# K and V of the first octet in rows of 4 KB: four transfers for two, and a branch of TensorE's loop for their sums

## The chip, the cores and the metric

The kernel runs on one core of a Trainium2 chip. The metric is the device time of one execution in microseconds (us), as the median of several runs. Engines are named as in the profile: PE (TensorE, matrix products), DVE (VectorE), ACT (ScalarE), POOL (GpSimd) and SP (SyncE, which here only issues transfers). Sixteen DMA engines move the data between HBM and the core's memory (SBUF); PE writes its results into PSUM.

## The reference

Linear attention with ReLU features, for 8 x 12 = 96 heads of 512 rows by 64 columns, all in float32:

```python
Q_feat = np.maximum(0, Q)                                   # Q, K, V: (8, 12, 512, 64)
K_feat = np.maximum(0, K)
KV = np.einsum('bhkd,bhkv->bhdv', K_feat, V)
K_sum = np.sum(K_feat, axis=2)
numerator = np.einsum('bhqd,bhdv->bhqv', Q_feat, KV)
denominator = np.einsum('bhqd,bhd->bhq', Q_feat, K_sum)
out = numerator / (denominator[:, :, :, None] + 1e-10)
```

Each head needs a 64 x 64 sum over its 512 keys, the sum of its keys, and then a product of its queries with both.

## The kernel before

**Tiles.** The 96 heads are taken in 12 octets of 8 heads (`NO = 12`). The view `Kr[o]` (and `Qr`, `Vr`, `Or`) is one octet of 1 MB, laid on 128 partitions with 32 rows of 64 numbers each (`RQ = 32`), which is one run of 8 KB per partition. A head thus covers 16 partitions.

**Loads.** Pool's queue loads Q, K and V and casts them to bf16 on the way (`load`, L174): 8 KB read and 4 KB written per row. Each input has `NI = 6` octets of buffers, and Pool's transfers take six semaphores (`lanes`) in turn; a transfer waits until the one before it on its lane has landed. Some transfers bring two octets. Only K and V of octet 0 come another way: SP issues them as they are, in float32, into the output buffers `o_sb[0]` and `o_sb[1]` (L267), each with a lane of its own. The helper `lane` deals out lanes in turn.

**Order.** There is no scheduler. `Order.op` (L58) records each instruction with the keys that it reads and writes, and adds the semaphore waits that follow from them. A transfer writes the key of its lane too (L65), so that a second transfer on a lane waits for the first. PE's work is a loop over `r` (L384), whose waits are written by hand and booked by `do.looped`.

**Per octet.** DVE turns K into masked features (`prep_k`, L191): for each row `kf` has two copies of 64 columns, one holding it where the partition belongs to an even head of a pair, the other where it belongs to an odd one. `prep_v` (L200 on ACT, L202 on DVE) does the same for V by a mask over 32 partitions, beside columns of ones. PE transposes Q (L389), multiplies for the denominators and numerators of the octet before (L382), sums K times V (L413), and transposes the numerators back (L422). The sums of an octet are 64 products over half of the partitions each: for each of 32 rows one over partitions 0 to 63 and one over 64 to 127, into two columns of banks of `ps_kv`. ACT copies the blocks on the diagonal into `kvd` (`evac_kv`, L218). DVE divides (`norm`, L245) into `o_sb`.

**Stores.** SP stores an octet of 1 MB at a time (L254). Every store's keys hold K's buffer of octet 11 (L253), so the first store waits until that load has landed, and all twelve follow one another after it.

**Start.** `body` issues K and V of octet 0 on SP, then on Pool the first loads, the identity, a block of memsets (L263), and the loads of octets 2 to 5. `setup` makes the masks on DVE from the identity (L297 to L302) and prepares octet 0, `begin` does the first turn around PE's loop, and `step(i)` the rest.

Of the kernel before, what the change touches and what calls it, by code (L numbers as in the profile page):

```python
# [96 lines left out]
def kernel(  # L97
# [19 lines left out]
    NI = 6  # L117
# [15 lines left out]

    ident = sb.tile([P, P], bf16, name="ident")
    ident32 = sb.tile([P, P], fp32, name="ident32")
    mask = sb.tile([P, 2, 2], fp32, name="mask")
    mask_h = sb.tile([P, 8, 2], fp32, name="mask_h")
    kf = sb.tile([P, RQ, 2, D], bf16, name="kf")
# [27 lines left out]
    def kv_src(o):  # L166
        if o == 0:
            return (o_sb[0], ("o", 0)), (o_sb[1], ("o", 1))
        return [(ins[n][:, o % NI].rearrange("p (r d) -> p r d", d=D), (n, o % NI)) for n in "kv"]
# [18 lines left out]
    def prep_k(o, s, halves=(0, 1), after=()):  # L188
        src, key = kv_src(o)[0]
        rs = slice(R * halves[0], R * halves[-1] + R)  # L190
        do.op("dve", lambda e: e.tensor_scalar(kf[:, rs, s, :], src[:, rs], scalar1=0.0, scalar2=mask[:, 0, s:s + 1],  # L191
                                               op0=Alu.max, op1=Alu.mult),
              reads=[key, ("mask", 0), *after], writes=[("kf", s, j) for j in halves])

    def prep_v(o, t, halves, who, sem=None):
        src, key = kv_src(o)[1]
# [6 lines left out]
        do.op(who, make, reads=[key, ("mask", 1), "vo1"], writes=[("vo", t, j) for j in halves], sem=sem)  # L203
# [11 lines left out]
    def evac_kv():  # L215
        for s in range(2):
            for c in range(2):
                do.op("act", lambda e: e.copy(  # L218
                    kvd[64 * c:64 * c + 64, s:8:2, c * D1:c * D1 + D1].rearrange("p (g t) d -> p g t d", t=2),
# [22 lines left out]
    def norm(o, j):  # L242
# [4 lines left out]
              reads=[("x", j), "rec"], writes=[("o", i, j)] if i > 1 else [("o", i, j), ("o", i)], sem=f"n{j}")  # L247
# [17 lines left out]
    def body():  # L265
        for c, X in enumerate((Kr, Vr)):
            do.op("sp", lambda e: e.dma_start(out=o_sb[c].rearrange("p r d -> p (r d)"), in_=X[0]),  # L267
                  writes=[("o", c)], dma=lane("sp"))
# [27 lines left out]
    def setup():  # L296
        do.op("dve", lambda e: e.tensor_copy(ident32, ident), reads=["ident"], writes=["ident32"])  # L297
        for c in range(2):
            do.op("dve", lambda e: e.tensor_reduce(
                out=mask_h[:, :, c], in_=ident32.rearrange("p (h b) -> p h b", h=8), op=Alu.add,  # L300
                axis=mybir.AxisListType.X), reads=["ident32"], writes=[("mh", c), "mask_h"])
# [31 lines left out]
    def begin():  # L333
        transposed(1)
        relu_q(0)
        relu_q(1)
        summed(1)
        evac_kv()
        prep_v(1, 1, (0,), "act", "a0")
        prepare(1)  # L340
# [37 lines left out]
    def products():  # L378
# [4 lines left out]

        with pe.Fori(0, NO + 2, 1) as r, pe.If(r > 0):  # L384
            with pe.If(r < NO + 1):
                pe.wait_ge(sems["rq"], r)
                pe.wait_ge(sems["q2"], r)
                for u in range(U):
                    x = pe.transpose(ps_qt[u // 8][:, u % 8, :], q2[:, u, :], ident)  # L389
                    if u % 8 == 7:  # L390
                        x.then_inc(sems["pe"], 1)
            with pe.If(r > 1):
# [13 lines left out]
            with pe.If(r < NO + 1):  # L406
                for g in range(2):
                    for s in ("a0", "d0") if g == 0 else ("d1",):
                        pe.wait_ge(sems[s], r)
                    for k in range(R):  # L410
                        for h in range(2):
                            ps = slice(64 * h, 64 * h + 64)
                            x = pe.matmul(  # L413
                                ps_kv[:, h, 0:2 * (D + 2)].rearrange("p (t d) -> p t d", t=2),
                                kf[ps, R * g + k, :, :].rearrange("p s d -> p (s d)"), vo[ps, R * g + k, :, 1:D4 - 1],
                                start=(g + k == 0), stop=(g == 1 and k == R - 1), skip_group_check=True)
                    x.then_inc(sems["pe"], 1)
            with pe.If(r > 1):
# [45 lines left out]
```

## Time and profile before

| what | value |
|---|---|
| median of 3 runs | 125.11 us (125.01 to 125.23) |
| profiled execution, whole | 125.09 us |
| its span | 123.3 us |
| DVE busy | 84.3 us (68%) |
| PE busy / weight loads | 81.1 us (66%) / 72.3 us (59%) |
| ACT busy | 76.3 us (62%) |
| POOL busy | 25.6 us (21%) |
| SP's queue (q1): packets | 2016, 14.68 MB |
| Pool's queue (q0): packets | 4832, 17.83 MB |
| HBM | 37.75 MB read, 12.58 MB written, 408 GB/s over the span |

The profile shows one execution by the hardware profiler. The span is what it covers; the run's own time is 1.8 us more. The page has the busy time of each engine, a strip of 40 slices of the span with busy tenths (for DMA the mean busy share of the 16 engines), the DMA queues, the chain of work that ended last, and the costliest groups of instructions. Further views of the trace answer for a stretch of time: the windows view gives each engine's busy time in a stretch, then PE's granted clock, the DMA share and the GB/s that were written; the timeline lists instructions in order, with the idle time before them and what ended it in brackets; the waits view adds up who waited for whom (total, times, longest). The trace also records each DMA packet with its queue, size, start and duration.

### The profile page before, as it was taken

The page shows a single profiled execution, that of the slowest core. Times are in us where ns is not written, and L with a number is a line of the kernel's source. Part 1 is how long each engine was busy: PE and PEld are TensorE (multiplying, and loading weights), DVE is VectorE, ACT ScalarE, POOL GpSimd, SP SyncE. Part 2 cuts the span into 40 slices and gives each one's busy share as a digit, 9 for nine tenths or more (in the row PEclk, how much of TensorE's full clock was granted, in tenths as well). Part 3 has the DMA queues.
Part 4 walks back from the last instruction along what each step waited for, and adds up shares of the span by engine and source line. Part 5 has one row for each costly group of instructions (what it writes and reads, how often), then busy time and mean ns, then how long its engine had stood idle before and what let it go on. Part 6 is the DMA issues. An engine that isn't in the chain of part 4 may idle for free.

```text
span 123.3 us, 3456 instructions
## 1 busy us (share of the span) xinstructions
PE 81.1 (66%) x1440; PEld 72.3 (59%) x1440; DVE 84.3 (68%) x149; ACT 76.3 (62%) x108; POOL 25.6 (21%) x64
## 2 busy tenths in 40 slices
PE   0000089797599896989989898989898884800000
PEld 0000089697289794979889797979696763700000
DVE  1252933555999879999999999999979577520000
ACT  0000751994698889979899999999996963000000
POOL 5888922001111013213331222100000000000000
PEclk9999999999679999999999999999999998695555
DMA  2999999999999999999999999999999999999991
GB/s 64 392 314 237 213 214 215 213 214 213 213 214 214 217 214 214 213 214 214 213 215 215 213 213 214 214 214 213 213 302 423 425 423 428 425 423 430 428 430 74
DMA packets 6852, 32.55 MB, mean 264 GB/s; under 512 B 704, under 2 KB 704, under 8 KB 5056
## 3 DMA queue, kind: packets, MB, share of 16 engines
q0 software_dynamic: 4832, 17.83, 72.0%
q1 hardware_dynamic: 2016, 14.68, 28.7%
q8 instruction: 1, 0.02, 0.1%
q14 instruction: 3, 0.02, 0.0%
HBM read 37.75 MB, written 12.58 MB: 408 GB/s over the span
## 4 chain that ended last, share of the span: by engine, by line
DMA 54%; DVE 18%; PE 8%; issue 5%; POOL 3%; POOLq 0%; DVEq 0%; SPq 0%
DMA v_sb<-in_V_dram 22%; DMA k_sb<-in_K_dram 20%; DMA q_sb<-in_Q_dram 12%; DVE o_sb L245 9%; PE ps_x L422 4%; DVE kf L191 4%; PE ps_kv L413 3%; DVE vo L202 2%; POOL q_sb L174 2%; DVE own L231 1%; DVE ot_sb L226 1%; POOL k_sb L174 1%; DVE den L237 1%; DVE q L206 1%; DVE rec L240 0%
## 5 line engine op out<-in xcount | busy, mean ns | idle before, releaser
L245 DVE TENSOR_TENSOR o_sb<-ps_x,rec 128x1024 f32<-128x1024 f32 x24 | 28.5, 1218 | 5.0 <-PE ps_x L422 4.4
L413 PE MATMUL ps_kv<-vo,kf 64*128 64x132 bf16 x768 | 27.0, 229 | 4.7 <-DVE vo L202 4.6
L413 PEld LDWEIGHTS ps_kv<-vo,kf 64*128 64x128 bf16 x768 | 25.0, 99 | 7.8 <-issue 7.8
L422 PE MATMUL ps_x<-ident,ot_sb 128*128 128x128 f32 x192 | 25.0, 286 | 1.7 <-DVE ot_sb L226 1.7
L226 ACT COPY ot_sb<-ps_x 128x1024 f32<-128x1024 f32 x23 | 22.4, 1015 | 4.7 <-PE ps_x L382 4.3
L210 ACT ACTIVATE qt<-ps_qt 128x1024 bf16<-128x1024 bf16 x24 | 23.5, 1040 | 1.9 <-PE ps_qt L389 1.9
L389 PE MATMUL ps_qt<-ident,q 128*128 128x128 bf16 x192 | 13.7, 229 | 15.8 <-DVE q L206 15.8
L422 PEld LDWEIGHTS ps_x<-ident,ot_sb 128*128 128x128 f32 x192 | 22.1, 147 | 3.2 <-issue 2.0
L191 DVE TENSOR_SCALAR kf<-k_sb,mask 128x1024 bf16<-128x1024 bf16 x44 | 18.6, 482 | 5.8 <-DMA k_sb<-in_K_dram 3.6
L389 PEld LDWEIGHTS ps_qt<-ident,q 128*128 128x128 bf16 x192 | 12.5, 103 | 16.1 <-issue 16.0
L218 ACT CAST kvd<-ps_kv 64x260 bf16<-64x260 f32 x48 | 18.0, 376 | 3.4 <-PE ps_kv L413 2.6
L382 PE MATMUL ps_x<-qt,kvd 128*128 128x256 bf16 x96 | 14.2, 284 | 3.3 <-DVE o_sb L245 3.2
L200 ACT ACTIVATE vo<-v_sb,mask 128x1024 bf16<-128x1024 bf16 x11 | 12.7, 1155 | 3.9 <-DMA v_sb<-in_V_dram 3.7
L202 DVE TENSOR_SCALAR vo<-v_sb,mask 128x2048 bf16<-128x2048 bf16 (+1 forms) x22 | 12.6, 615 | 0.0
L382 PEld LDWEIGHTS ps_x<-qt,kvd 128*128 128x128 bf16 x96 | 7.9, 101 | 6.5 <-DVE o_sb L245 5.1
L174 POOL DMA_DIRECT2D v_sb<-in_V_dram x11 | 6.5, 588 | 22.2 <-DMA q_sb<-in_Q_dram 8.6
L206 DVE COPY q<-q_sb 128x2048 bf16<-128x2048 bf16 x12 | 7.7, 646 | 2.8 <-PE ps_qt L389 2.1
L174 POOL DMA_DIRECT2D k_sb<-in_K_dram x9 | 6.2, 685 | 15.5 <-DMA k_sb<-in_K_dram 10.3
L174 POOL DMA_DIRECT2D q_sb<-in_Q_dram x10 | 6.3, 632 | 13.9 <-DMA q_sb<-in_Q_dram 7.1
L200 ACT ACT_TABLE_LOAD x1 | 1.3, 1283 | 12.5 <-DMA o_sb<-in_V_dram 12.5
L382 PE MATMUL ps_kv<-kvd,qt 128*128 128x16 bf16 x192 | 7.0, 179 | 0.9 <-ACT kvd L218 0.9
L382 PEld LDWEIGHTS ps_kv<-kvd,qt 128*128 128x128 bf16 x192 | 6.2, 96 | 1.3 <-ACT kvd L218 1.3
(20 smaller groups left out, 29.5 us busy)
## 6 DMA issues: line engine op xcount, KB each, us to landing
out_dram<-o_sb SPq DMA_DIRECT2D x12, 1024.0 KB, 16.3
v_sb<-in_V_dram POOLq DMA_DIRECT2D x11, 512.0 KB, 15.6
q_sb<-in_Q_dram POOLq DMA_DIRECT2D x8, 512.0 KB, 14.5
k_sb<-in_K_dram POOLq DMA_DIRECT2D x7, 512.0 KB, 14.4
q_sb<-in_Q_dram POOLq DMA_DIRECT2D x2, 1024.0 KB, 17.0
k_sb<-in_K_dram POOLq DMA_DIRECT2D x2, 1024.0 KB, 20.4
o_sb<-in_K_dram SPq DMA_DIRECT2D x1, 1024.0 KB, 6.5
o_sb<-in_V_dram SPq DMA_DIRECT2D x1, 1024.0 KB, 11.0
```

The costliest lines, as they stand in the source:

```text
L174: do.op("pool", lambda e: e.dma_start(out=ins[n][:, i:i + m], in_=src, single_packet=True), writes=[(n, x % NI) for x in octets], dma=lane ...
L191: do.op("dve", lambda e: e.tensor_scalar(kf[:, rs, s, :], src[:, rs], scalar1=0.0, scalar2=mask[:, 0, s:s + 1], op0=Alu.max, op1=Alu.mult) ...
L200: make = lambda e: e.activation(to, src, Act.Copy, scale=m)
L202: make = lambda e: e.tensor_scalar(to, src, scalar1=m, scalar2=None, op0=Alu.mult)
L210: do.op("act", lambda e: e.activation(qt[:, j * (U // 2):(j + 1) * (U // 2)], ps_qt[j], Act.Relu), reads=[("pq", j)], writes=[("qt", j)], ...
L218: do.op("act", lambda e: e.copy(kvd[64 * c:64 * c + 64, s:8:2, c * D1:c * D1 + D1].rearrange("p (g t) d -> p g t d", t=2), ps_kv[64 * s:64 ...
L226: do.op(who, lambda e: e.copy(to, src) if who == "act" else e.tensor_copy(to, src), reads=[("x", j)], writes=[("ot", j)], sem=f"t{j}")
L245: do.op("dve", lambda e: e.tensor_tensor(o_sb[i][:, rs], ps_x[j].rearrange("p (r d) -> p r d", d=D), rec[:, rs].unsqueeze(2).to_broadcast( ...
L382: return pe.matmul(out_, lhsT, rhs, start=True, stop=True, skip_group_check=True)
L389: x = pe.transpose(ps_qt[u // 8][:, u % 8, :], q2[:, u, :], ident)
L413: x = pe.matmul(ps_kv[:, h, 0:2 * (D + 2)].rearrange("p (t d) -> p t d", t=2), kf[ps, R * g + k, :, :].rearrange("p s d -> p (s d)"), vo[p ...
L422: x = pe.transpose(ps_x[u // 8][:, u % 8 * P:u % 8 * P + P], ot[:, u].rearrange("p h c -> p (h c)"), ident32)
```

## The change

K and V of octet 0 are seen through another view, `Kf` and `Vf`: four heads on 128 partitions, 16 rows (4 KB) on each. Two transfers of 0.5 MB fill the two halves of `o_sb[0]` for K, two more those of `o_sb[1]` for V. The lanes are written out: both halves of K on `sl0`, V's on `sl1` and `sl2`. As a head now covers 32 partitions in octet 0, its K mask is `mask_f` (halves of 64 partitions), and the sums of a group of four heads run over all 128 partitions: 32 products in a branch of its own in PE's loop for `r < 2`, ahead of the branch for `r > 1`, into which the sums of the later octets move. `evac_kv(True)` writes octet 0's blocks to where their heads belong. The masks are made by three reductions on DVE as before, of another shape.

```diff
@@ -131,10 +131,13 @@
 
     Qr, Kr, Vr, Or = [view(X, RQ * D) for X in (Q, K, V, out)]
 
+    Kf, Vf = [view(X, R * D) for X in (K, V)]
+
     ident = sb.tile([P, P], bf16, name="ident")
     ident32 = sb.tile([P, P], fp32, name="ident32")
     mask = sb.tile([P, 2, 2], fp32, name="mask")
     mask_h = sb.tile([P, 8, 2], fp32, name="mask_h")
+    mask_f = sb.tile([P, 2], fp32, name="mask_f")
     kf = sb.tile([P, RQ, 2, D], bf16, name="kf")
     vo = sb.tile([P, RQ, 2, D4], bf16, name="vo")
     kvf = sb.tile([P, 8 * 2 * D1], bf16, name="kvd")
@@ -165,8 +168,8 @@
 
     def kv_src(o):
         if o == 0:
-            return (o_sb[0], ("o", 0)), (o_sb[1], ("o", 1))
-        return [(ins[n][:, o % NI].rearrange("p (r d) -> p r d", d=D), (n, o % NI)) for n in "kv"]
+            return [(o_sb[c], [("in", c, 0), ("in", c, 1)]) for c in range(2)]
+        return [(ins[n][:, o % NI].rearrange("p (r d) -> p r d", d=D), [(n, o % NI)] * 2) for n in "kv"]
 
     def load(n, *octets):
         o, i, m = octets[0], octets[0] % NI, len(octets)
@@ -186,21 +189,22 @@
                     load(n, x)
 
     def prep_k(o, s, halves=(0, 1), after=()):
-        src, key = kv_src(o)[0]
+        src, keys = kv_src(o)[0]
         rs = slice(R * halves[0], R * halves[-1] + R)
-        do.op("dve", lambda e: e.tensor_scalar(kf[:, rs, s, :], src[:, rs], scalar1=0.0, scalar2=mask[:, 0, s:s + 1],
+        m = mask[:, 0, s:s + 1] if o else mask_f[:, s:s + 1]
+        do.op("dve", lambda e: e.tensor_scalar(kf[:, rs, s, :], src[:, rs], scalar1=0.0, scalar2=m,
                                                op0=Alu.max, op1=Alu.mult),
-              reads=[key, ("mask", 0), *after], writes=[("kf", s, j) for j in halves])
+              reads=[*[keys[j] for j in halves], ("mask", 0) if o else "mask_f", *after], writes=[("kf", s, j) for j in halves])
 
     def prep_v(o, t, halves, who, sem=None):
-        src, key = kv_src(o)[1]
+        src, keys = kv_src(o)[1]
         rs = slice(R * halves[0], R * halves[-1] + R)
         to, src, m = vo[:, rs, t, 2:D + 2], src[:, rs], mask[:, 1, t:t + 1]
         if who == "act":
             make = lambda e: e.activation(to, src, Act.Copy, scale=m)
         else:
             make = lambda e: e.tensor_scalar(to, src, scalar1=m, scalar2=None, op0=Alu.mult)
-        do.op(who, make, reads=[key, ("mask", 1), "vo1"], writes=[("vo", t, j) for j in halves], sem=sem)
+        do.op(who, make, reads=[*[keys[j] for j in halves], ("mask", 1), "vo1"], writes=[("vo", t, j) for j in halves], sem=sem)
 
     def copy_q(o):
         do.op("dve", lambda e: e.tensor_copy(q2.rearrange("p u f -> p (u f)"), ins["q"][:, o % NI]),
@@ -212,11 +216,16 @@
 
     KVD = [("kvd", s, c) for s in range(2) for c in range(2)]
 
-    def evac_kv():
+    def evac_kv(first=False):
         for s in range(2):
             for c in range(2):
+                to = kvd[64 * c:64 * c + 64, :, c * D1:c * D1 + D1]
+                if first:
+                    to = to.rearrange("p (g s t) d -> p s g t d", g=2, s=2)[:, s]
+                else:
+                    to = to.rearrange("p (g t s) d -> p s g t d", g=2, s=2)[:, s]
                 do.op("act", lambda e: e.copy(
-                    kvd[64 * c:64 * c + 64, s:8:2, c * D1:c * D1 + D1].rearrange("p (g t) d -> p g t d", t=2),
+                    to,
                     ps_kv[64 * s:64 * s + 64, :, 0:2 * (D + 2)].rearrange(
                         "p g (t d) -> p g t d", t=2)[:, :, :, c:c + D1]),
                     reads=[("pk", 0), ("pk", 1)], writes=[("kvd", s, c)], sem="ev" if s + c == 2 else None)
@@ -244,7 +253,7 @@
         rs = slice(16 * j, 16 * j + 16)
         do.op("dve", lambda e: e.tensor_tensor(o_sb[i][:, rs], ps_x[j].rearrange("p (r d) -> p r d", d=D),
                                                rec[:, rs].unsqueeze(2).to_broadcast([P, 16, D]), op=Alu.mult),
-              reads=[("x", j), "rec"], writes=[("o", i, j)] if i > 1 else [("o", i, j), ("o", i)], sem=f"n{j}")
+              reads=[("x", j), "rec"], writes=[("o", i, j)] if i > 1 else [("o", i, j), ("in", i, 0), ("in", i, 1)], sem=f"n{j}")
 
     def store(o):
         i = (o + 2) % NOUT
@@ -263,9 +272,12 @@
         do.op(who, lambda e: e.memset(ap, value), writes=[key] if isinstance(key, (str, tuple)) else key)
 
     def body():
-        for c, X in enumerate((Kr, Vr)):
-            do.op("sp", lambda e: e.dma_start(out=o_sb[c].rearrange("p r d -> p (r d)"), in_=X[0]),
-                  writes=[("o", c)], dma=lane("sp"))
+
+        ways = [lanes["sp"][x] for x in (0, 0, 1, 2)]
+        for c, X in enumerate((Kf, Vf)):
+            for g in range(2):
+                do.op("sp", lambda e: e.dma_start(out=o_sb[c][:, R * g:R * g + R].rearrange("p r d -> p (r d)"), in_=X[g]),
+                      writes=[("in", c, g)], dma=ways[2 * c + g])
         load("q", 0)
         memset("pool", ident, 0.0, "ident")
         do.op("pool", lambda e: e.affine_select(out=ident, in_=ident, compare_op=Alu.not_equal, fill=1.0, base=0,
@@ -295,10 +307,12 @@
 
     def setup():
         do.op("dve", lambda e: e.tensor_copy(ident32, ident), reads=["ident"], writes=["ident32"])
-        for c in range(2):
-            do.op("dve", lambda e: e.tensor_reduce(
-                out=mask_h[:, :, c], in_=ident32.rearrange("p (h b) -> p h b", h=8), op=Alu.add,
-                axis=mybir.AxisListType.X), reads=["ident32"], writes=[("mh", c), "mask_h"])
+        do.op("dve", lambda e: e.tensor_reduce(
+            out=mask_f, in_=ident32.rearrange("p (s b) -> p s b", s=2), op=Alu.add, axis=mybir.AxisListType.X),
+            reads=["ident32"], writes=["mask_f"])
+        do.op("dve", lambda e: e.tensor_reduce(
+            out=mask_h, in_=ident32.rearrange("p (h b) -> p h b", h=8).unsqueeze(2).to_broadcast([P, 8, 2, 16]),
+            op=Alu.add, axis=mybir.AxisListType.X), reads=["ident32"], writes=["mask_h"])
         do.op("dve", lambda e: e.tensor_reduce(
             out=mask[:, 0, :], in_=mask_h[:, :, 0].rearrange("p (a s) -> p s a", s=2), op=Alu.add,
             axis=mybir.AxisListType.X), reads=["mask_h"], writes=[("mask", 0)])
@@ -335,7 +349,7 @@
         relu_q(0)
         relu_q(1)
         summed(1)
-        evac_kv()
+        evac_kv(True)
         prep_v(1, 1, (0,), "act", "a0")
         prepare(1)
 
@@ -381,6 +395,15 @@
         def mm(out_, lhsT, rhs):
             return pe.matmul(out_, lhsT, rhs, start=True, stop=True, skip_group_check=True)
 
+        def await_rows(g, r):
+            for s in ("a0", "d0") if g == 0 else ("d1",):
+                pe.wait_ge(sems[s], r)
+
+        def summand(h, ps, k, start, stop):
+            return pe.matmul(ps_kv[:, h, 0:2 * (D + 2)].rearrange("p (t d) -> p t d", t=2),
+                             kf[ps, k, :, :].rearrange("p s d -> p (s d)"), vo[ps, k, :, 1:D4 - 1],
+                             start=start, stop=stop, skip_group_check=True)
+
         with pe.Fori(0, NO + 2, 1) as r, pe.If(r > 0):
             with pe.If(r < NO + 1):
                 pe.wait_ge(sems["rq"], r)
@@ -389,6 +412,12 @@
                     x = pe.transpose(ps_qt[u // 8][:, u % 8, :], q2[:, u, :], ident)
                     if u % 8 == 7:
                         x.then_inc(sems["pe"], 1)
+            with pe.If(r < 2):
+                for g in range(2):
+                    await_rows(g, r)
+                    for k in range(R):
+                        x = summand(g, slice(0, P), R * g + k, k == 0, k == R - 1)
+                    x.then_inc(sems["pe"], 1)
             with pe.If(r > 1):
                 pe.wait_ge(sems["ev"], r)
                 for u in range(U):
@@ -403,19 +432,14 @@
                            kvd[:, h, 1:2 * D + 1], q[:, :, h, :])
                     if h % 4 == 3:
                         x.then_inc(sems["pe"], 1)
-            with pe.If(r < NO + 1):
-                for g in range(2):
-                    for s in ("a0", "d0") if g == 0 else ("d1",):
-                        pe.wait_ge(sems[s], r)
-                    for k in range(R):
-                        for h in range(2):
-                            ps = slice(64 * h, 64 * h + 64)
-                            x = pe.matmul(
-                                ps_kv[:, h, 0:2 * (D + 2)].rearrange("p (t d) -> p t d", t=2),
-                                kf[ps, R * g + k, :, :].rearrange("p s d -> p (s d)"), vo[ps, R * g + k, :, 1:D4 - 1],
-                                start=(g + k == 0), stop=(g == 1 and k == R - 1), skip_group_check=True)
-                    x.then_inc(sems["pe"], 1)
-            with pe.If(r > 1):
+                with pe.If(r < NO + 1):
+                    for g in range(2):
+                        await_rows(g, r)
+                        for k in range(R):
+                            for h in range(2):
+                                x = summand(h, slice(64 * h, 64 * h + 64), R * g + k, g + k == 0,
+                                            g == 1 and k == R - 1)
+                        x.then_inc(sems["pe"], 1)
                 pe.wait_ge(sems["t0"], r)
                 pe.wait_ge(sems["t1"], r)
                 for u in range(U):
```

## The prediction, made before the changed kernel was run

> **What bounds the kernel.** I read the profile page first, for the row of DMA shares:
>
> ```profile
> span 123.3 us, 3456 instructions
> DVE  1252933555999879999999999999979577520000
> DMA  2999999999999999999999999999999999999991
> q0 software_dynamic: 4832, 17.83, 72.0%
> q1 hardware_dynamic: 2016, 14.68, 28.7%
> ```
>
> After the first slice of 3.1 us the 16 DMA engines are full to the last slice, while DVE has gaps at both ends. The page's chain of waits leads through DVE and V loads, but it ends at the last norm; what follows it is only transfers. So next, who waits at the end (waits of SP, then DVE's timeline):
>
> ```profile
> SPq L254 <- DMA k_sb<-in_K_dram: 86.1, 1, 86.1
> ...
> SPq L435 <- DMA out_dram<-o_sb: 12.7, 1, 12.7
> ```
> ```profile
> 106.22 2.55 DVE L245 TENSOR_TENSOR o_sb<-ps_x,rec 128x1024 f32<-128x1024 f32 x2 [2.19 <-PE ps_x L422]
> ```
>
> Computing ends at 108.77; SP then waits 12.7 us for stores alone. All twelve stores are held back until octet 11's K has landed (87.8), so 37.75 MB of reads and 12.58 MB of writes pass through one full stream. The windows show where it has holes:
>
> ```profile
> 2.00:3.00 1.00, 0.00 (x0) 0.00 (x0) 0.23 (x2) 0.00 (x0) 0.93 (x4) 1.00 0.78 139
> 3.00:4.00 1.00, 0.00 (x0) 0.00 (x0) 0.74 (x3) 0.00 (x0) 1.00 (x3) 1.00 1.06 451
> 4.00:5.00 1.00, 0.00 (x0) 0.00 (x0) 0.00 (x0) 0.00 (x0) 0.89 (x4) 1.00 1.00 410
> ...
> 120.00:121.00 1.00, 0.00 (x0) 0.00 (x0) 0.00 (x0) 0.00 (x0) 0.00 (x0) 0.50 0.64 270
> 121.00:122.00 1.00, 0.00 (x0) 0.00 (x0) 0.00 (x0) 0.00 (x0) 0.00 (x0) 0.50 0.12 49
> ```
>
> None between 3 and 120. The last microsecond belongs to few engines. The trace's packet records say why: the final store's 16 completions lie at 120.8 to 121.6 for fourteen engines, then 121.97 and 122.22. The last engine has been about 1.1 us behind since the start, where one 16 KB instruction fetch held it from 5.08 to 6.13. Thus: **time = start of the stream + packet time + holes, on the slowest DMA engine.** Computing counts only if it leaves a queue empty or the last store late.
>
> **Part 1: the loads, the only part on the path.** The timeline of the start:
>
> ```profile
> 0.96 0.39 SPq L267 DMA_DIRECT2D o_sb<-in_K_dram  x1
> 1.40 0.42 SPq L267 DMA_DIRECT2D o_sb<-in_V_dram  x1
> 1.46 0.66 POOL L174 DMA_DIRECT2D q_sb<-in_Q_dram  x1 [1.00 <-SPq L427]
> ```
>
> K and V (8 rows of 8 KB on each engine, 309 ns a row) start at 2.25 to 2.9. q0's packets (Pool's queue, 8 KB read, 324 ns) appear only at 5.7 to 6.3; then both queues alternate packet by packet. K's completions are at 5.39 to 5.67, the fetch-delayed engine's at 7.37; V's at 10.0 to 10.6, and 12.34.
>
> After, the first half of K (K0) is 8 rows of 4 KB per engine. Both halves of K use lane `sl0`, so SP's second issue waits until K0 is complete, and both V issues stand behind it; nothing else is on SP until the stores, 80 us later. K0's last row ends near 2.25 + 1.2 (the first packet's time there) + 7 x 0.155 = 4.5, or 4.3 on the eight engines that start at 2.9; the engine with the fetch may be near 6.2. K1's issue is then at 4.6 to 6.3.
>
> Does the stream break between K0 and q0? That is the question of this change, and the trace does not show q0 alone. I judge it by another switch of queues: the first store is issued at 87.91, yet on the normal engines its first packet is at 91.38, just as the eight rows of Pool's last load end, without a gap, though K's first packet needed 1.3 us from its issue. A newly filled queue thus seems to wait for about eight packets already taken up. Early likewise: q0 starts after 9 rows of K and V on eight engines, 10 on most others. Eight packets before 5.7 is about 3.2 to 3.6, so q0 was probably there before K0's last row at 4.3 to 4.5, and follows it directly. A read still has its latency (K's first packet took 1.0 to 1.2 us): the hole is 0 to 0.75 us. The engine with the fetch fills it with the fetch, and it is the last one by 0.25 us (122.22 against 121.97), so the first 0.25 us cost nothing. I take 0.05 us net, near the switch at 91.38, which shows no hole.
>
> Extra packets: K and V become 32 rows per engine instead of 16, and two more completions. The nearest row for a packet's fixed part is a 4-byte semaphore packet: mostly 9 ns on this queue, 22 on Pool's. 16 x 9 = 0.14, 2 x 9 = 0.02; bounds 0 and 0.4.
>
> The Trainium skill (DMA: Bandwidth & Descriptors, "Why small descriptors are slow (HBM only)") gives a fixed cost of about 3 cycles per packet; at the 850 MHz of its "Specifications" that is an estimate of 0.06 us for 16 packets. No run here has 4 KB rows on this queue.
>
> Alternating: a row of SP's queue between Pool's takes 322 ns instead of 309, Pool's 322 instead of 324. Before, some 6 rows per engine alternate; after, K1, V0 and V1, 24. 18 x 11 ns is 0.2 at most, but the pairs advance every 0.62 us against 0.614 apart: 0.08.
>
> Sum on the path: 0.14 + 0.02 + 0.08 + 0.05 = **+0.3 us**.
>
> **Part 2: what starts late, and its cover.** K1 waits 1.3 us plus eight Pool packets (2.5), so its first row is at 8.4 to 10.1. A 4 KB row now takes its turn with an 8 KB read: 0.155 + 0.322 = 0.48 us, 3.8 us for eight. K is complete at 12 to 15 (before 7.4), V at 20 to 23 (before 12.3). Pool's ring does not run dry: q0, k1, q1, v1 hold 32 packets per engine, the next loads come at 11.82.
>
> DVE's `prep_v` needs both halves of V, and `copy_q(0)`, hence PE's first transposes, stand behind it. The first `ps_kv` sums move from 21.3 to about 29 to 32. DVE idles 2.66 and 0.91 us for K loads at 29.07 and 43.78:
>
> ```profile
> 29.07 1.74 DVE L191 TENSOR_SCALAR kf<-k_sb,mask 128x1024 bf16<-128x1024 bf16 x4 [2.66 <-DMA k_sb<-in_K_dram]
> ```
>
> These loads land no earlier, so 3.6 us are absorbed and the last norm ends 5 to 7 us late, 113.8 to 115.8. A 1 MB transfer alone takes 4.4 to 4.7 from issue to completion (K's); the last store would be ready at 120.5 at the latest, but its turn ends at 122.2 anyway. Cost: nothing, with 1.7 us of cover left. Pool's loads wait for their lanes, 15 us ahead of the data; the first that needs anything of octet 0 is issued at 34.15 (it overwrites q0, copied by 27).
>
> **Part 3: PE, masks, evacuation.** 64 half-height products become 32 full ones. Later octets do 64 in 2.07 us (48.91), 32 ns for 132 columns, so the two halves already run side by side: the gain is 0 to 1.8 us, and off the path. PE has one test more and one fewer per turn. DVE's three reductions become three others before its K wait; the four evacuations keep their sizes. All this is ahead of waits that end last elsewhere: zero, or with its cover gone 0.3 us on a chain with 1.7 us to spare. PE's program grows by 64 products and their weight loads; a second 16 KB fetch on the slowest engine would cost 1.05 us, on any other at most a little.
>
> **Forecast.** The profiled execution took 125.09, 1.8 beyond its span, which stays; the median is 125.11. 125.09 + 0.3 = **125.4 us**; this case alone reaches from 125.1 to 126.0 (hole of 0.75 net of 0.25, packets at 0.4).
>
> **Rivals.**
> *The stream breaks* (slower). If q0's packets truly cannot come before 5.7 to 6.15 per engine, the engines stand idle from 4.3 to 4.5 until then: 1.4 to 1.7, less 0.25 covered, plus 0.25 for packets: about +1.5, 126.6. It decides as soon as the hole exceeds 0.25. For: no q0 packet is seen before 5.4. Against: the gapless switch at 91.38.
>
> The Trainium skill speaks for this rival (same page, "Bandwidth", its rule to batch transfers to 1 MiB, with some 2.0 us fixed per transfer from "Anatomy of one DMA"): the wait lays one such part bare, an estimate of up to +2.0 us. This trace shows no such gap between K and V, issued without a wait.
>
> *Computing reaches the end* (slower). If V lands past 25, the last norm passes 117.6 and its store ends past 122.2; from there each microsecond counts. V at 26.5 gives 126.9. Against: it needs 3.5 us beyond my latest time.
>
> *The late engine catches up* (faster). If the 16 KB fetch falls into a hole of its engine, that engine is no longer last, and the two behind most (121.97, 121.57) set the end: 0.25 to 0.65 less, against 0.25 for packets, so at best 124.7. For: K0's queue is short just then. Against: an engine without a hole pays the fetch in full.
>
> *The split does nothing*: SP's rows keep their bandwidth and only order changes: 125.1.
>
> **How the numbers follow.** About 0.25 us (0.2%) is what a measurement of this kernel can tell from no change. Forecast 0.60: of it 0.38 above that bound, 0.21 within, 0.01 below. Broken stream 0.17, computing at the end 0.06: all slower. Late engine 0.12: 0.11 faster, 0.01 same. Split without effect 0.05: 0.04 same, 0.01 faster. Together faster 0.13, same 0.26, slower 0.61. The range 124.95 to 126.7 leaves out about a tenth on each side: most of the late engine's case, and the dearer ends of the two slower rivals.
>
> **What would show it.** Right: DMA shares of 9 from the second slice on; SP's second K issue at 4.6 to 6.3; V landing at 20 to 23; DVE's last norm at 113 to 116; last completion near 122.5. A window below 0.9 between 4 and 7 us, and the end later by as much, means the broken stream. SP's wait for the last stores shrinking below 5 us means computing. One engine no longer behind the rest in the last microsecond means the late engine. I am wrong altogether if the time changes by over 0.5 us with the stream full and the slowest engine as far behind as before.

## The result, and the profile after

The changed kernel takes 126.18 us, the median of six runs from 125.89 to 127.14. The kernel before takes 125.10 in its six runs beside it, 125.01 to 125.23. The ratio is 1.010, with a 95% interval of 1.0061 to 1.0138. That is 1.1 us slower, inside the range given, but over three times the 0.3 us that the sum gave. Not only the median moved: the spread of the runs grew from 0.2 us to 1.25. The profiled execution took 126.2 with a span of 124.4. (Ratios leave out runs over 1.5% above the fastest of the same kernel, which below are two of eight with the loop from 1, eight of thirteen with the loads first and one of six with the memsets on DVE; medians and ranges are of all runs.)

The page of the changed kernel:

```profile
span 124.4 us, 3392 instructions
DVE  1200703625999999999999999999999929270000
DMA  3999999999999999999999999999999999999980
GB/s 105 228 220 274 286 275 232 216 212 212 212 211 220 215 216 211 213 212 211 217 217 213 215 211 212 212 211 215 220 328 427 419 424 419 429 437 424 432 377 26
q0 software_dynamic: 4832, 17.83, 71.6%
q1 hardware_dynamic: 2304, 14.68, 28.6%
```

SP's queue has 288 packets more: 256 rows and two times 16 completions. The row of DMA shares is as full as before. Still the span is 1.1 us longer. Its timeline, for the start:

```profile
0.96 3.89 SPq L279 DMA_DIRECT2D o_sb<-in_K_dram  x2
...
4.91 1.13 SPq L279 DMA_DIRECT2D o_sb<-in_V_dram  x2
...
13.08 2.54 DVE L195 TENSOR_SCALAR kf<-o_sb,mask_f 128x2048 bf16<-128x2048 f32 x2 [9.27 <-DMA o_sb<-in_K_dram]
...
20.73 2.07 DVE L206 TENSOR_SCALAR vo<-o_sb,mask 128x2048 bf16<-128x2048 f32 x2 [5.11 <-DMA o_sb<-in_V_dram]
```

The second issue waits inside the first line (the waits view has 3.2 us for it). K is there at 13.0 where it was at 7.4, V at 20.5 where it was at 12.3. Windows of the same trace (the last two columns are the DMA share and GB/s written):

```profile
3.00:4.00 1.00, 0.00 (x0) 0.00 (x0) 0.78 (x3) 0.00 (x0) 1.00 (x3) 1.00 1.10 320
4.00:5.00 1.00, 0.00 (x0) 0.00 (x0) 0.00 (x0) 0.00 (x0) 0.89 (x4) 1.00 1.06 201
5.00:6.00 1.00, 0.00 (x0) 0.00 (x0) 0.00 (x0) 0.00 (x0) 0.71 (x6) 1.00 0.92 168
6.00:7.00 1.00, 0.00 (x0) 0.00 (x0) 0.00 (x0) 0.00 (x0) 0.77 (x5) 1.00 1.11 193
...
121.00:122.00 1.00, 0.00 (x0) 0.00 (x0) 0.00 (x0) 0.00 (x0) 0.00 (x0) 0.50 0.24 98
122.00:123.00 1.00, 0.00 (x0) 0.00 (x0) 0.00 (x0) 0.00 (x0) 0.00 (x0) 0.50 0.06 25
```

There is no hole between 3 and 7 us. But look at the GB/s: with Pool's casting packets alone the later stream writes 211 to 220 (the GB/s row of the page, from the eighth slice to the 29th), and here 168 to 201. The engines are busy and slow. The packet records show how. Pool's first packet comes at 3.85, right behind K's first half. A packet of Pool takes 324 ns in the full stream. Up to 12 us 57 of them take over 345 ns, the longest 819 and 1314, where the kernel before has one such packet. (The records do not name the engine of a packet; which engine is late is read from the completions.) The 16 completions of q0 lie between 6.31 and 8.90; before, between 10.35 and 11.11. Four engines come out of this phase late, and the latest does not catch up: it is 1.95 us behind the median at the first store, at 96 us, and 1.94 at the last; before, 1.23 at both. The final store's completions lie at 120.9 to 121.7 for twelve engines, then at 121.98, 122.19, 122.39 and 123.34. So the median engine ends 0.4 us later than before (121.40 against 120.99), and the last one 1.1 us (123.34 against 122.22). The time follows the last one.

At the end, computing is still no part of it. DVE's last line and SP's waits:

```profile
108.72 2.51 DVE L254 TENSOR_TENSOR o_sb<-ps_x,rec 128x1024 f32<-128x1024 f32 x2 [2.19 <-PE ps_x L446]
```
```profile
SPq L459 <- DMA out_dram<-o_sb: 11.3, 1, 11.3
```

The last norm ends at 111.23 where it ended at 108.77, and SP waits 11.3 us for stores alone.

### The profile page after: what moved, and what is told of

Read it like the earlier page. It is cut to its first block, busy times and chain, and to the rows that moved or that the text cites. A ratio compares the mean times of both kernels' runs of the same rounds, so it can differ in the third digit from the quotient of the medians.

```text
span 124.4 us, 3392 instructions
## 1 busy us (share of the span) xinstructions
PE 77.6 (62%) x1408; PEld 70.5 (57%) x1408; DVE 84.0 (67%) x149; ACT 76.0 (61%) x108; POOL 22.7 (18%) x64
## 4 chain that ended last, share of the span: by engine, by line
DVE 35%; PE 34%; DMA 15%; issue 2%; ACT 1%; SPq 1%; DVEq 0%
DVE o_sb L254 22%; PE ps_kv L403 20%; DMA o_sb<-in_V_dram 12%; PE ps_x L446 12%; DVE vo L206 8%; DVE own L240 3%; DMA o_sb<-in_K_dram 3%; PE ps_qt L412 1%; ACT kvd L227 1%; DVE ot_sb L235 1%; SPq L279 1%; DVE q L210 1%; PE ps_kv L396 0%; DVE den L246 0%; DVE rec L249 0%
## 5 line engine op out<-in xcount | busy, mean ns | idle before, releaser
L403 PE MATMUL ps_kv<-vo,kf 64*128 64x132 bf16 (+1 forms) x736 | 25.6, 221 | 5.1 <-DVE vo L206 5.1
L403 PEld LDWEIGHTS ps_kv<-vo,kf 64*128 64x128 bf16 (+1 forms) x736 | 23.9, 95 | 7.9 <-issue 7.2
L412 PEld LDWEIGHTS ps_qt<-ident,q 128*128 128x128 bf16 x192 | 12.3, 102 | 24.3 <-issue 24.1
L396 PE MATMUL ps_x<-qt,kvd 128*128 128x256 bf16 x96 | 12.8, 272 | 0.3 <-DVE o_sb L254 0.3
L195 DVE TENSOR_SCALAR kf<-o_sb,mask_f 128x2048 bf16<-128x2048 f32 x2 | 2.5, 1309 | 9.3 <-DMA o_sb<-in_K_dram 9.3
## 6 DMA issues: line engine op xcount, KB each, us to landing
out_dram<-o_sb SPq DMA_DIRECT2D x12, 1024.0 KB, 15.3
```

Of the source, the lines that this page charges most:

```text
L396: return pe.matmul(out_, lhsT, rhs, start=True, stop=True, skip_group_check=True)
L403: return pe.matmul(ps_kv[:, h, 0:2 * (D + 2)].rearrange("p (t d) -> p t d", t=2), kf[ps, k, :, :].rearrange("p s d -> p (s d)"), vo[ps, k, ...
```

## The experiments

What was open: which part of the change makes engines late. The candidates were the wait, the 4 KB rows, PE's longer program with its 16 KB fetch, and later Pool's own work, SP's issues, and how early Pool's packets start. The table collects the readings of all kernels: Pool's first packet, the number of its packets over 345 ns up to 12 us, the median and the last of the 16 completions of the final store (all from one profiled execution each), and the median time of the runs with the ratio to the kernel before beside it. A single execution is one sample, and the runs of a kernel with slow packets spread over 1 us and more.

| kernel | Pool's first | over 345 ns | median end | last end | time, us | ratio (95%) |
|---|---|---|---|---|---|---|
| before | 5.70 | 1 | 120.99 | 122.22 | 125.10 | 1 |
| changed | 3.85 | 57 | 121.40 | 123.34 | 126.18 | 1.0061 to 1.0138 |
| own lane | 5.11 | 15 | 120.99 | 122.62 | 125.50 | 1.0004 to 1.0023 |
| one transfer each | 5.78 | 1 | 121.19 | 122.75 | 125.60 | 1.0016 to 1.0038 |
| before, V waits | 5.43 | 4 | 121.02 | 122.14 | 125.22 | 0.9988 to 1.0006 |
| loop from 1 | 3.97 | 63 | 121.81 | 123.17 | 126.06 | 1.0033 to 1.0077 |
| loads first | 3.78 | 56 | 122.36 | 124.17 | 127.04 | see below |
| V waits, 4 KB | 5.38 | 0 | 121.07 | 122.66 | 125.50 | 1.0008 to 1.0025 |
| 64 partitions | 4.63 | 8 | 124.01 | 125.32 | 128.27 | 1.0194 to 1.0250 |
| q0 first | 3.08 | 44 | 122.16 | 122.96 | 126.19 | 1.0060 to 1.0094 |
| 2 KB first | 3.10 | 102 | 122.35 | 123.69 | 126.65 | 1.0094 to 1.0147 |
| memsets on DVE | 3.71 | 57 | 122.53 | 124.13 | 127.20 | 1.0102 to 1.0185 |
| rest after q0 | 3.85 | 39 | 121.24 | 124.01 | 126.91 | 1.0110 to 1.0141 |
| issues early, 8 KB | 3.06 | 26 | 122.02 | 122.68 | 125.74 | 1.0027 to 1.0055 |

In every row the profiled execution's time is its last end plus 2.86 to 3.03 us. That is the first thing shown: the time goes with the last DMA engine.

### The wait taken out

```diff
-"sp": [f"sl{i}" for i in range(3)]
+"sp": [f"sl{i}" for i in range(4)]
-        ways = [lanes["sp"][x] for x in (0, 0, 1, 2)]
+        ways = [lanes["sp"][x] for x in (0, 3, 1, 2)]
```

> The changed kernel with a fourth lane on SP, so that K's second half does not wait for its first; rows stay at 4 KB. Theory W (the wait makes Pool's first packets run alone from 3.4 us, some of them slow, and one engine late): the stream starts as in the kernel before, the last of the 16 completions of the final store is about 1.2 us behind the median one again, and the time is 125.1 to 125.5 us. Theory R (the 4 KB rows themselves cost it): the time stays at 126 to 126.4 us. Theory P (PE's longer program makes the instruction fetch dearer): also 126 to 126.4.

Measured: 125.50 (125.14 to 125.61), ratio 1.0014. The last completions in its windows, to be held against the changed kernel's two lines above:

```profile
121.00:122.00 1.00, 0.00 (x0) 0.00 (x0) 0.00 (x0) 0.00 (x0) 0.00 (x0) 0.50 0.10 41
122.00:123.00 1.00, 0.00 (x0) 0.00 (x0) 0.00 (x0) 0.00 (x0) 0.00 (x0) 0.50 0.02 8
```

After 122 only a third of the bytes is left (8 against 25 GB/s), and the last end is 122.62. Most of the loss, some 0.9 of 1.1 us, goes away with the wait, while the 4 KB rows, the branch of PE, the masks and the evacuation all stay. Together they cost what is left, 0.17 us by the ratio (0.05 to 0.3 by its interval). The time is at the upper end of what theory W gave, and one thing is not as it said: the last engine is 1.6 us behind the median and not 1.2.

### The split taken out as well

```diff
-        ways = [lanes["sp"][x] for x in (0, 0, 1, 2)]
+        ways = [lanes["sp"][x] for x in (0, 1)]
...
-            for g in range(2):
-                do.op("sp", lambda e: e.dma_start(out=o_sb[c][:, R * g:R * g + R].rearrange("p r d -> p (r d)"), in_=X[g]),
-                      writes=[("in", c, g)], dma=ways[2 * c + g])
+            do.op("sp", lambda e: e.dma_start(out=o_sb[c].rearrange("p (g r) d -> p g (r d)", g=2),
+                                              in_=X[0:2].rearrange("g p f -> p g f")),
+                  writes=[("in", c, 0), ("in", c, 1)], dma=ways[c])
```

> The changed kernel with one transfer for K and one for V, each of two 4 KB rows per partition, so that neither splitting nor waiting is left, but the small rows and PE's branch are. Theory W: 125.1 to 125.5 us, the same as with a lane of its own. Theory R or P: 126 to 126.4 us. If splitting into four transfers costs something by itself, this one is below the kernel with its own lane by over 0.2 us.

Measured: 125.60, ratio 1.0027, just above theory W's 125.1 to 125.5 and far from the 126 of the others. So the rows of 4 KB with everything that belongs to them cost 0.2 to 0.3 us (ratios 1.0014 and 1.0027), and four transfers instead of two cost nothing more. The median end is 121.19 here and 120.99 with four: 0 to 0.2 us above the kernel before. The last engine adds to it: it is 1.6 us behind the median in both, 1.2 before. Why rows of 4 KB make it later, with one slow packet of Pool in this run, is not shown.

### The wait put into the kernel before

```diff
-                  writes=[("o", c)], dma=lane("sp"))
+                  writes=[("o", c)], dma=lanes["sp"][0])
```

> The kernel before (rows of 8 KB, two transfers) with one edit: V is put on K's lane and so waits for K. Pool's first packets then run alone from about 5.6 us until V comes, at about 9 us or later. Theory W in its first form (slow because Pool is still writing the descriptors of its next loads until 4.3 us): 125.1 to 125.4 us, no slow packets. Theory W in its second form (slow because nothing but Pool's packets is in the queue while its memsets run, until 8 to 11 us): 125.6 to 126.4 us, with packets of 350 ns and more between 5.6 and 9 us. Theories R and P: 125.1 us.

```profile
0.96 0.39 SPq L267 DMA_DIRECT2D o_sb<-in_K_dram  x1
7.42 0.33 SPq L267 DMA_DIRECT2D o_sb<-in_V_dram  x1
```

SP's part of its timeline: V is issued 6 us later than before. Measured: 125.22, ratio 0.9997 (0.9988 to 1.0006). This separates two things that looked alike. A wait that keeps SP's queue empty for microseconds cost nothing here: Pool's packets fill the stream, all but alone and at 324 ns, from 5.4 us to past 9. The second form of the theory, that Pool's packets are slow whenever they run alone beside its memsets, falls with it.

### PE's loop started at 1

```diff
-        with pe.Fori(0, NO + 2, 1) as r, pe.If(r > 0):
+        with pe.Fori(1, NO + 2, 1) as r, pe.If(r > 0):
```

> The changed kernel with PE's loop started at 1, so that its first, empty turn with its jump over the body is gone. If the 16 KB instruction fetch at 4.24 us is PE's and belongs to that jump, it goes or moves. Theory P (the fetch on one engine, together with Pool's first packets there, makes that engine 2 us late): 125.3 to 125.7 us, and no engine over 1 us behind the median at the end. Theory W without the fetch: the other late engines remain, about 0.9 us behind, 125.8 to 126.2. If the fetch is not PE's, nothing changes: 126.2.

The 16 KB fetch moved from 4.24 to 31.1 us, so it is PE's. The time did not follow: 126.06, from 125.35 to 127.6. At the end four engines are late (122.77, 123.10, 123.12, 123.17), and the packet records have 1409 ns as the longest packet without any fetch near. Theory P is out as the main cause: without the fetch there are 63 slow packets, and 126.06 lies in the 125.8 to 126.2 that theory W gave for this case. How much the fetch adds in the changed kernel is not told, as the two intervals overlap (1.0033 to 1.0077 and 1.0061 to 1.0138).

### Pool's loads issued earlier

```diff
         load("q", 0)
+        for n in "kqv":
+            load(n, 1)
         memset("pool", ident, 0.0, "ident")
```

(The same two lines are taken out behind the identity.)

> The changed kernel with Pool's loads k1, q1 and v1 issued right behind q0, ahead of the identity; all four are then issued by about 3.7 us instead of 4.3. Theory F (Pool's queue is slow while it is still being filled: its first packets run at 3.4 to 4 us, before the next loads are written): fewer packets over 345 ns between 3 and 9 us than the changed kernel's 57, the latest engine less than 2 us behind at q0's end, and 125.4 to 125.9 us with less spread than 125.9 to 127.1. Theory A (Pool's packets are slow whenever they run alone so early, whatever is written): no change, 126 to 126.5 us. Theory X (packets of Pool collide with SP's issue of the second half of K and of V, 4 to 6 us): no change either.

The 13 runs fall into two groups: five at 125.03 to 125.41 and eight at 126.97 to 128.05, with nothing between, so the table has no ratio for it. The profiled execution, from the upper group, has 56 packets over 345 ns, up to 1822, and in the windows of 4 to 7 us it writes 131, 135 and 147 GB/s, less still than the changed kernel's 201, 168 and 193. Theory F expected fewer slow packets and less spread; there are as many, and the spread is larger. The 126 to 126.5 us of theories A and X lie between the groups, where no run is. The lower group shows that the same program can also pass this start without any loss; what decides between the two, no reading here shows.

### The wait behind twice the work

```diff
-        ways = [lanes["sp"][x] for x in (0, 1)]
+        ways = [lanes["sp"][x] for x in (0, 0)]
```

(Against the kernel with one transfer each.)

> 4 KB rows in one transfer for K and one for V, and V waits for K: the wait is kept, but behind 2.5 us of work per engine instead of 1.2, so that Pool's packets start at about 5.4 us, when all of its first four loads are written. Theory F: no slow packets, 125.4 to 125.7 us as without the wait (125.6). Theory X (collision with SP's later issues, then at 7 to 9 us): slow packets there and 126 us or more. If rows of 4 KB and a wait make it slow together, however the queue is filled: also 126 or more.

Measured: 125.50, ratio 1.0016, and no packet over 345 ns, as theory F had it. Rows of 4 KB and a wait do no harm together when 2.5 us of work per engine stand ahead of Pool's queue instead of 1.2. Theory X in its first form (any issue of SP among Pool's packets) is not borne out either: V's issue is at 7.83, in the middle of them.

### Large rows, early start

```diff
-            do.op("sp", lambda e: e.dma_start(out=o_sb[c].rearrange("p r d -> p (r d)"), in_=X[0]),
-                  writes=[("o", c)], dma=lane("sp"))
+            for g in range(2):
+                ps = slice(64 * g, 64 * g + 64)
+                do.op("sp", lambda e: e.dma_start(out=o_sb[c][ps].rearrange("p r d -> p (r d)"), in_=X[0][ps]),
+                      writes=[("o", c), ("half", c, g)] if g else [("half", c, g)],
+                      dma=lanes["sp"][(0, 0, 1, 2)[2 * c + g]])
```

(`prep_v` of octet 0 waits for V's first half as well.)

> The kernel before with K and V each cut into two transfers over 64 partitions, rows of 8 KB kept, and the changed kernel's lanes: K's second half waits for its first, V stands behind. The first transfer is again 0.5 MB, so Pool's packets start alone at about 4 us, with large rows and without any change of PE, DVE or masks. Theory F: 125.8 to 126.8 us, with some 50 packets of Pool over 345 ns before 9 us and several late engines. Theory R2 (it takes the 4 KB rows and the wait together): 125.1 to 125.4 us and no slow packets.

Measured: 128.27, ratio 1.022. This one does not answer its question. The transfers of 64 partitions are slow themselves: most of their 8 KB rows, 199 of 256, take 490 to 670 ns in place of 309. Over 309 ns that adds up to 3.5 us per engine, enough for the 3.0 us by which the median end is later. Pool's packets started alone at 4.63 and ran well (8 over 345 ns), but behind rows at half the speed.

### q0 ahead of everything

```diff
+        load("q", 0)
         for c, X in enumerate((Kr, Vr)):
             do.op("sp", lambda e: e.dma_start(out=o_sb[c].rearrange("p r d -> p (r d)"), in_=X[0]),
-                  writes=[("o", c)], dma=lane("sp"))
-        load("q", 0)
+                  reads=[("q", 0)], writes=[("o", c)], dma=lane("sp"))
```

> The kernel before with SP's two transfers (8 KB rows, as before) held back until q0 has landed. Pool's queue then starts the stream with nothing ahead of it, which shows when its first packet can come at the earliest, and how its packets run from cold. Theory L (a queue of Pool that starts with little of SP's work in front has no lead, and its packets come late one by one until SP's packets come in between): first packet of q0 at 3.2 to 3.6 us, dozens of packets over 345 ns until about 10 us, several late engines, and 126.2 to 128 us (0.5 to 1 us for the later start, the rest for the late engines). Rival (small rows of SP must be ahead for it): no slow packets, 125.7 to 126.2 us for the later start alone.

```profile
2.00:3.00 1.00, 0.00 (x0) 0.00 (x0) 0.23 (x1) 0.00 (x0) 0.93 (x4) 1.00 0.41 49
3.00:4.00 1.00, 0.00 (x0) 0.00 (x0) 0.74 (x3) 0.00 (x0) 1.00 (x3) 1.00 0.74 98
4.00:5.00 1.00, 0.00 (x0) 0.00 (x0) 0.00 (x0) 0.00 (x0) 0.89 (x4) 1.00 1.00 197
```

Windows of its trace. Pool's first packet comes at 3.08: with an empty stream it is there 2.6 us earlier than the 5.70 at which it appeared in the kernel before. This bears out the reading that the forecast rested on: q0 could have been there at 3.08, and in the kernel before it came only after rows that the engines had taken up already. The Trainium skill (DMA: Bandwidth & Descriptors, "Specifications") gives about 1 us to the first byte for this kind of queue; the trace agrees, with 0.95 us from the end of Pool's issue at 2.13.

The time, 126.19, is for the most part that of a late start: the median end is 1.2 us later (122.16 against 120.99), of which the time shows 1.0. Of the 44 packets over 345 ns, 26 are in the first 1.5 us, when reads begin; from 4.5 on there are 18 in 5.5 us, although Pool's packets run alone until 10. So each side is half right: there are dozens of slow packets, as theory L had it, but no SP packets are needed to bring Pool's queue up to speed, and the start leaves no engine late.

The 16 KB fetch is now at 2.58, inside the hole, and no engine is late for it: at the first store no engine completes more than 0.23 us behind the median, where the kernel before has one 1.23 behind. The last end, 0.8 us behind the median, comes from the stores themselves.

### A smaller first piece

```diff
+                if c + g == 0:
+                    for x in range(2):
+                        do.op("sp", lambda e: e.dma_start(
+                            out=o_sb[0][:, 8 * x:8 * x + 8].rearrange("p r d -> p (r d)"),
+                            in_=X[0][:, 512 * x:512 * x + 512]),
+                              writes=[("in", 0, 0)], dma=lanes["sp"][0])
+                    continue
```

(What stands behind it uses a fourth lane, so that it waits for nothing of its own.)

> The changed kernel with K's first group cut once more, into two transfers of 256 KB with 2 KB rows; the second waits for the first, and everything else of SP stands behind it. The work ahead of Pool's queue shrinks from 1.2 to 0.6 us per engine. Theory L: Pool's packets start at about 3.5 us with still less lead, after a hole of about 0.3 us; 126.3 to 128 us, at least as many slow packets as the changed kernel's 57. Rival (how much work stands ahead does not matter): as the changed kernel, 126.2, plus 0.1 for the added packets.

Measured: 126.65, ratio 1.012, with 102 packets over 345 ns. The direction is that of theory L: less work ahead, more slow packets, a longer time. Some 0.4 us of the window from 3 to 4 us is a plain hole (its DMA share is 0.60), and what the slow packets take beyond 324 ns adds up to 15.3 us, 0.96 per engine: together about the 1.36 us by which the median end is later. This run alone does not tell whether it is the shorter lead or the late start that makes the packets slow.

### Pool's memsets moved away

```diff
-            memset("pool", ones[:, 8 * c:8 * c + 8, :, 0:D + 2:D1], 0.0, "vo1")
+            memset("dve", ones[:, 8 * c:8 * c + 8, :, 0:D + 2:D1], 0.0, "vo1")
```

(The sixteen memsets to 1.0 likewise.)

> The changed kernel with the 20 memsets of the V tile moved from Pool to DVE, where they are done by about 4 us; Pool is then idle but for eight small memsets while its first packets run, and issues the next loads at 5 to 6 us. Rival M (Pool's own memsets hold up its queue's packets): no slow packets and 125.3 to 125.7 us. Theory L (the lead decides, not what Pool does): slow packets as in the changed kernel and 126 to 127 us.

Measured: 127.20 (126.07 to 128.14), and 57 packets over 345 ns, up to 1907. It is not Pool's memsets. (On DVE they last until 4.85 us, not 4.)

### SP silent while Pool's packets start

```diff
-                      writes=[("in", c, g)], dma=ways[2 * c + g])
-        load("q", 0)
+                      reads=[("q", 0)] if c + g else [], writes=[("in", c, g)], dma=ways[2 * c + g])
+                if c + g == 0:
+                    load("q", 0)
```

> The changed kernel with SP's other three issues (K's second half, V's halves) held back until q0 has landed, at 6.3 us or later. K's first half is as before it, so Pool's packets start alone at 3.8 us, but SP issues nothing between 4.3 and 6 us. Theory X (Pool's packets are held up while SP's issues fall among them): no slow packets from 4.5 to 6.3 us, fewer than 25 in all, 125.3 to 125.9 us. Theory S (small rows ahead and an early start are enough, whatever SP issues): about 50 slow packets until SP's rows come in between, 126 to 127 us.

Measured: 126.91, ratio 1.0125. Theory X is out: SP issues nothing between 1.4 us and 8.8, and the time is no better than the changed kernel's. There are 39 slow packets, fewer than theory S's 50 and more than theory X's 25; the time is in theory S's range. Here the bulk is nearly unharmed (median end 121.24), and one engine ends 2.8 us behind it. The fetch at 4.20 and a Pool packet of 833 ns may both be that engine's; the records do not show it:

```profile
121.00:122.00 1.00, 0.00 (x0) 0.00 (x0) 0.00 (x0) 0.00 (x0) 0.00 (x0) 0.50 0.20 82
122.00:123.00 1.00, 0.00 (x0) 0.00 (x0) 0.00 (x0) 0.00 (x0) 0.00 (x0) 0.50 0.08 33
123.00:124.00 1.00, 0.00 (x0) 0.00 (x0) 0.00 (x0) 0.00 (x0) 0.00 (x0) 0.50 0.04 16
```

A DMA share of 0.06 is one engine of 16 for a whole microsecond: from 122.7 on that engine works alone.

### SP's issues among Pool's packets, large rows

```diff
     def setup():
...
+        for c, X in enumerate((Kr, Vr)):
+            do.op("sp", lambda e: e.dma_start(out=o_sb[c].rearrange("p r d -> p (r d)"), in_=X[0]),
+                  reads=[("mask", 0)], writes=[("o", c)], dma=lane("sp"))
         prep_k(0, 0)
```

(The same loop at the start of `body` is taken out.)

> The kernel before, 8 KB rows, with SP's two issues held back until DVE's masks are done (3.8 us). As in the run with q0 first, Pool's packets start the stream alone at 3.1 us, with no small rows anywhere; but SP's issues now fall at 3.9 to 4.8 us, among them, instead of at 6.8. Theory X: more slow packets than the 44 of the run with q0 first, above all between 4.5 and 8 us, and 126.4 to 127.5 us. Theory S: as with q0 first, 126.0 to 126.3 us.

Measured: 125.74, ratio 1.0041, and 26 packets over 345 ns, fewer than with q0 first. That is faster than either theory gave. SP's issues at 3.8 to 4.8 us do no harm that shows, and without small rows ahead Pool's early start leaves no engine late. The median end is 1.0 us later than before, for the hole at the start, but the last end only 0.5 us, since the fetch falls into the hole here too. Both this run and the one with q0 first thus lose less in time than in their median ends.

## Why the prediction was right in sign and short in size

**What bounds the kernel** held throughout: the stream of transfers, on its slowest engine. All times follow the last end.

**The number** is inside the range by luck. The forecast's own case reached from 125.1 to 126.0, and 126.18 lies beyond it. The range went further up only for the broken stream and for computing at the end, and neither happened. What did happen, more lag of the slowest engine in a full stream, was on no list, and none of the named signs describes it.

**The hole between K's first half and q0** was the question, and the answer given was right. There is none. q0 was ready at 3.08 (the run with q0 first) and follows directly. The rival of the broken stream does not occur: the wait alone, put into the kernel before, costs nothing (0.9988 to 1.0006). The Trainium skill's fixed 2.0 us per transfer (DMA: Bandwidth & Descriptors, "Anatomy of one DMA", a section on transfers that Pool issues) is thus not laid bare here.

**Packets and alternation** were put at 0.24 us. The two kernels without the wait show 0.17 and 0.33 us in time, 0 and 0.2 in the median end. That term stands in size. The rows agree with its working: a 4 KB row takes 159 ns alone and 172 in alternation, an 8 KB row 309 and 322, so that two of the small ones cost 9 or 22 ns more than one large one; with 4 such pairs alone and 12 in alternation that is about 0.3 us per engine.

**The slowest engine** is the step that failed. The forecast took its lag of 1.2 us from the trace of before, let it cover the first 0.25 us of any hole, and left the lag itself as it was. It is 1.94 in the changed kernel, 0.7 more. The sum of 0.3 was close to the 0.4 by which the median engine is later, but that is luck in part: what the 57 slow packets take beyond 324 ns adds up to 7.2 us, 0.45 per engine, and the working had no slow packets. The missing 0.7 is the lag. Some 0.4 of it goes with the 4 KB rows, since the three kernels that have them and few slow packets or none have a lag of 1.6; the rest comes with the wait. The working asked only whether the stream breaks, and not whether it runs at full speed once Pool's packets are alone: the second K transfer's wait opens 4 to 8 us to them alone, right behind a small first piece, and there the latest engine is 2.5 us behind the median when q0 has landed, the fetch of 0.93 us possibly included.

**The late engine catching up** was rated as the way to a gain. The mechanism exists, in the two kernels where the fetch falls into a hole. In the changed kernel there is no hole at the fetch (4.24 to 5.17), as the argument against it said.

**Part 2** held in its reading: K's arrival at 13.0 was forecast at 12 to 15, V's at 20.5 at 20 to 23, the sums' end at 28.7, a little ahead of 29 to 32. The last norm was forecast 5 to 7 us late and is 2.5 late: of the 7.4 us by which the first sums end later, 4.9 are absorbed and not 3.6. DVE's waits for loads of K and Q, 4.2 us before, are gone. It cost nothing, as said. **Part 3** cost nothing that can be told from the 0.2 to 0.3 us of the rows. PE's program grew by the 32 products of the new branch, not by the 64 that the working counts.

**What stays open.** All six kernels with dozens of slow packets and several or very late engines have a small first transfer of small rows ahead and Pool's packets alone right behind it, and no other kernel has both. That these two make the engines late is argued from this, not shown: the run that was to part them, 64 partitions, had slow rows of its own. The fetch, Pool's memsets, SP's issues and the order of Pool's loads are not needed for it; and neither the wait, nor the small rows, nor an early start with nothing ahead does it alone. Why some packets then take 350 to 1900 ns, why one program passes the same start once at 125.1 and once at 127.5, and why 4 KB rows alone make the last engine 0.4 us later, was not found. No version here beats the kernel before: the best, its V waiting for K, is equal to it.

## What to carry to other kernels

When transfers are the bound, read the completions engine by engine: a transfer is done when the last of 16 engines is, and an engine that fell behind in the full stream stayed behind here, 1.95 us at the first store and 1.94 at the last. A wait between two transfers can cost nothing while another queue has work ready (0.9988 to 1.0006 here), but then ask how fast that queue runs when it is alone, above all in the first microseconds. Cutting the first load to have it sooner made it later here, 13.0 for 7.4 us: the second piece went to the back of the other queue's packets.

## What was not expected of the hardware

- A newly filled queue waited for some eight packets per engine that were taken up before it: q0's first packet is at 5.70 behind SP's rows, and at 3.08 with nothing ahead, and 2.62 us are eight to nine rows of 309 ns.
- One instruction fetch of 16 KB takes 0.93 to 1.36 us of one DMA engine. In the kernel before, one engine is about 1.2 us behind from there to the end; with the fetch in a hole, at 2.57, no engine is more than 0.53 behind at the first store.
- Transfers over 64 partitions moved most of their 8 KB rows in 490 to 670 ns each, those over 128 partitions in 309.
